# Pool-input products placed inside the attention, pool openings beside products, and another half first in a w_down tile

## The chip, the cores and the metric

The kernel runs on one core of one Trainium2 chip. The metric is device time in microseconds (us), the median of several runs; lower is better. Engines are named as in the profile: PE (TensorE matmul), PEld (TensorE weight load), DVE (VectorE), ACT (ScalarE), POOL (GpSimd), SP (SyncE, which issues the DMAs).

## What is computed

Two layers of a diffusion backbone on 512 latent and 128 context tokens, with the same weights, D_MODEL 1024. The reference, cut to one layer:

```python
def trunk_layer(x, mod, lp, attend):
    h = modulate(rmsnorm(x, lp['g_ffn1']), m[0], m[1])
    x = x + 0.5 * m[2] * swiglu(h, lp['w_ffn1_gate'], lp['w_ffn1_up'], lp['w_ffn1_down'])
    n = modulate(rmsnorm(x, lp['g_mix']), m[3], m[4])
    proj = n @ lp['w_in']
    q, k, v, u_pool, u_conv, gate_b, gate_c, merge = jnp.split(proj, IN_OFFSETS, axis=-1)
    ...
    a = attend(q, k, v).transpose(0, 2, 1, 3).reshape(B, L, ATTN_DIM)
    pl = multiscale_pool(u_pool, lp['w_pool'], lp['pool_scale'])
    cv = gate_b * short_conv(gate_c * u_conv, lp['w_conv'], lp['b_conv'])
    g_a, g_p, g_c = jnp.split(jax.nn.sigmoid(merge), N_BRANCH, axis=-1)
    merged = (g_a * (a @ lp['w_br_attn']) + g_p * (pl @ lp['w_br_pool'])
              + g_c * (cv @ lp['w_br_conv']))
    x = x + m[5] * (merged @ lp['w_out'])
    h = modulate(rmsnorm(x, lp['g_ffn2']), m[6], m[7])
    x = x + 0.5 * m[8] * swiglu(h, lp['w_ffn2_gate'], lp['w_ffn2_up'], lp['w_ffn2_down'])
```

`attend` is a neighbourhood attention with 8 heads of 64 (windows of 8 rows by 16 columns plus 128 cached context keys) for latent tokens, and a full attention over 128 tokens for context. `multiscale_pool` takes means over windows of 2, 4, 8 and 16 tokens; `short_conv` is a depthwise convolution over 3 tokens.

## The kernel before

The body is Python that writes every engine's instruction list by a planner (`Sched`). Strands of work are generators; each `yield ACT(n)`, `PE(n, 3)` and the like asks for an engine with an estimated cost, and the planner grants the request that can start first, and of those the one of the smaller priority number. So the order on each engine is fixed when the program is built; on the chip an instruction waits by semaphores for its data and its buffers only. `yield event` holds a strand in the planner's time. Rings hand out buffers: 8 PSUM banks (`BANK`), 5 temporaries, 4 weight staging buffers (`RAW`), 4 pairs of split weights (`HL`).

All 640 tokens are columns; activations lie as 128 features by 640 tokens. A float32 operand is kept as a high and a low part, and every product is three matmuls (`mm3`, L302 to L304). Weights arrive in pieces of 512 KB over SP and are split into the parts `wh` (ACT, L307) and `wl` (DVE, L310) ahead of use.

The main strand (priority 5) goes through a layer: first FFN in three chunks (`ffn`), token mixing (`mix`), second FFN. In a chunk of `ffn` the gate and up products of 8, 8 and 6 feature tiles come first (`unit`; its products for the first token half, `n21`, end last), then eight w_down tiles (`dn`), each for token half 0 and then half 1; `dn` reads the activations `gh` and `gl` of all the chunk's feature tiles.

`mix` opens a memory pool `att` and starts the attention's strands at priorities about 2: per pair of heads `s_master` transposes q and k (L1344), multiplies scores (L1321, L1322) and starts the softmax (DVE, ACT L1310); `t_master` transposes its rows (L1415, and L1437 for context tokens), and multiplies values (L1326, L1327). Beside them main multiplies the q, k and v columns of w_in, which go through `qk_post` (POOL, L1200 to L1213), and four gate pieces (`xgate_post`). Then main waits until scores, values and copies of all four pairs are through (`yield sm_done`, `yield tm_done`, `at_ev`, `xev`), and `att` closes. Next it opens the pool `pc` and multiplies the eight pieces `u` (pool input), `x`, `c` and `b` (convolution), two of each, of 128 columns of w_in by all tokens, half by half (`gemm`, 384 and 256 tokens). Their results are copied or multiplied out of PSUM (`nat_copy`, `nat_mul`, `conv_out`), and `pool_mean`, `pool_map` and `conv` work on them, mostly on DVE. When these are done (`for ev in done`), `pc` closes and `mrg` opens: sigmoids of the gates (L1746, L1753), six more gate groups (`gate`), branch products, the merge (`br_post`, DVE), and w_out products (`outp`), which read the merged rows `mg`.

`acc` are two tiles of 384 columns in which the norms sum squares (L655).

Of the kernel before, what the change touches and what calls it, by code (L numbers as in the profile page):

```python
# [183 lines left out]
def POOL(n):  # L184
    return ("pool", 0.16 + n * 0.0021)
# [80 lines left out]
def body(ctx: ExitStack, tc: tile.TileContext, a, outs):  # L266
# [20 lines left out]
    small = const.tile([128, 32, 4], F32, name="small")  # L287
    acc = [const.tile([128, 384], F32, name=f"acc{h}") for h in range(2)]

# [541 lines left out]
    def ffn(l, i, ops, close, nxt, nxt_b):  # L831
# [167 lines left out]
        for ci, (c0, c1) in enumerate(CHUNKS):  # L999
            nk = c1 - c0  # L1000
            last = ci == len(CHUNKS) - 1
            gev = [[Ev(), Ev()] for _ in range(nk)]
            for f in range(nk):
                if ci or f >= NW:
                    yield from unit(f, gev[f], f == nk - 1)
                    continue
                w2 = []
                for _ in range(2):
                    w2.append((yield from w_take()))
                done = [S.spawn(whole(h, f, w2, gev[f]), 4 + h + 0.1 * f) for h in range(2)]  # L1010

                def end(w2=w2, done=done, f=f):
                    for ev in done:
                        yield ev
                    for w in w2:
                        w_free(w)
                    S.set(tail[f])

                S.spawn(end(), 0)
            xe, op_n, nt_ev = [[None] * KD] * 2, None, None  # L1020
            halves = HB if nxt_b or not last else HA
            if last and nxt:
                nt_ev = Ev()
                xe, op_n = nxt(nt_ev) if nxt_b else nxt()
            W = []
            for d in range(KD):
                w = yield from w_take()
                yield from dn(w, nk, d, halves[0], gev, xe[0][d])
                if last and d == 0 and nxt_b:

                    for ev in side:
                        yield ev
                    es2.close()
                    np_ = es.enter_context(tc.tile_pool(name="ntmp", bufs=1))
                    nt = [np_.tile([128, 4, 320], F32, name=f"nt{j}") for j in range(4)]
                    S.set(nt_ev, (nt, [t[:, 6:8].rearrange("p a (b t) -> p (a b) t", b=2) for t in g2]))
                if last and d >= 4:
                    W.append(w)
                    continue
                yield from dn(w, nk, d, halves[1], gev, xe[1][d])  # L1040
                w_free(w)
            for d, w in enumerate(W, 4):
                yield from dn(w, nk, d, halves[1], gev, xe[1][d])
                w_free(w)
# [9 lines left out]
    def mix(l, op, nxt):  # L1054
# [8 lines left out]

        with tc.tile_pool(name="att", bufs=1) as tpool:

# [425 lines left out]

            S.spawn(misc(), 2)
            S.spawn(klo_zero(), 2)
            S.spawn(ck_strand(), 2)
# [22 lines left out]
            for w in w1:  # L1517
                w_free(w)
            for u in (1, 2, -1, 3):
                w0 = yield from take2()  # L1520
                for b in range(5):
                    (p,) = yield from b_form(w0, b)
                    if u < 0:
                        S.spawn(v_post(p, 1, b), 2.4)
                    else:
                        S.spawn(qk_post(p, u, b), 2)
                for w in w0:
                    w_free(w)
            xev = []
            for i in range(2):  # L1530
                wait = v_ev[1] if i == 0 else tr_ev[3]
                for c in range(2):
# [5 lines left out]
                    w_free(w)  # L1538
            yield sm_done
            yield tm_done  # L1540
            for p_ in range(4):
                for ev in at_ev[p_]:
                    yield ev
            for ev in xev:
                yield ev

        if True:
            sp = [t[:, SPARE:].rearrange("p (a t) -> p a t", t=NT) for t in NN]
            pl = [sp[0][:, 0:2], sp[0][:, 2:4]]
# [3 lines left out]

            def nat(h, t, p):

                v = t[:, NL0:NL0 + 512].rearrange("p (r j c) -> p j r c", r=8, j=4)
                if h == 0:
                    yield v[:, 0:3], p[:, 0:384].rearrange("p (j r c) -> p j r c", j=3, r=8)
                else:
                    yield v[:, 3], p[:, 0:128].rearrange("p (r c) -> p r c", r=8)  # L1560
                    yield t[:, NC0:NC0 + 128], p[:, 128:256]

            with tc.tile_pool(name="pc", bufs=1) as pc:
                u = pc.tile([128, 2, NAT], F32, name="u")
                xs = pc.tile([128, 2, NAT], F32, name="xs")
# [10 lines left out]
                LO, HI = NC0, NL0 + 512  # L1576
                u_ev = [[Ev(), Ev()] for _ in range(2)]
                x_ev = [[Ev(), Ev()] for _ in range(2)]
# [14 lines left out]

                def pads():
                    yield POOL(200)
                    for t in (u, xs):
                        for c0, c1 in ((0, NC0), (NC0 + 128, NL0), (NL0 + 512, NAT)):
                            nc.gpsimd.memset(t[:, :, c0:c1], 0.0)
                    S.set(pad_ev)

                def nat_copy(dst, p, c, h, ev):
                    yield pad_ev
                    for nv, blk in nat(h, dst[:, c], p):
                        yield ACT(384 if h == 0 else 128)
                        copy(nv, blk)
                    S.give(BANK, p)
                    S.set(ev)

                def nat_mul(p, c, h, ev):
# [7 lines left out]
                def conv_out(p, c, h):  # L1617
                    yield y_ev[c]
                    n = HW[h]
                    t = yield TMP  # L1620
                    for (nv, blk), (_, tblk) in zip(nat(h, u[:, c], p), nat(h, u[:, c], t)):
                        yield DVE(384 if h == 0 else 128)
# [16 lines left out]
                def pool_mean(c):  # L1639
# [4 lines left out]
                    yield ld_ev  # L1644
                    uc = u[:, c]
                    yield from shift_add(s2, uc, 0, 1, NAT, RA)
# [44 lines left out]
                def conv(c):  # L1691
                    for ev in c_ev[c] + pm_ev:
                        yield ev
                    z = xs[:, c]
                    yo = y[:, c, LO:HI]
                    yield DVE(HI - LO)
# [9 lines left out]

                done = []
                S.spawn(loads(), 2)
                S.spawn(pads(), 1)
                for c in range(2):  # L1710
                    S.spawn(pool_mean(c), 2)
                    done.append(S.spawn(pool_map(c), 2))
                    S.spawn(conv(c), 2)
                for kind in "uxcb":
                    for c in range(2):
                        w = yield from w_take()
                        for h in range(2):
                            p = yield BANK
                            yield from gemm(p, w, 0, n2, HA[h], op[h])
                            if kind == "u":  # L1720
                                S.spawn(nat_copy(u, p, c, h, u_ev[c][h]), 2)
                            elif kind == "x":
                                S.spawn(nat_copy(xs, p, c, h, x_ev[c][h]), 2)
                            elif kind == "c":
                                S.spawn(nat_mul(p, c, h, c_ev[c][h]), 2)
                            else:
                                done.append(S.spawn(conv_out(p, c, h), 2))
                        w_free(w)
                for ev in done:
                    yield ev  # L1730

            if True:
                rp = es.enter_context(tc.tile_pool(name="mrg", bufs=1))
                wm0 = cnt["take"]
                items = [(r, hf) for r in ADA[l, "mix"][1] for hf in range(2)]
                side = S.spawn(ada(l, items, rp, lambda j: w_done[wm0 + 30 * j // (8 * len(items))]), 6)
                sg = [rp.tile([128, 2, NT], F32, name=f"sg{i}") for i in range(3)]
                mg = [sp[1][:, 2:6], rp.tile([128, 4, NT], F32R, name="mg1")]
                sga_ev = [Ev(), Ev()]
# [8 lines left out]

                def sg_post(p, dp, i, c, h):
                    if dp:  # L1750
                        yield br_ev[dp - 1][c][h]
# [42 lines left out]
                def branch(w, dp, c, h):  # L1794
                    banks = []
                    for i, (src, k0, nk) in enumerate((((ahi, alo), 0, 4), (pl, 4, 2), (cv, 6, 2))):
# [3 lines left out]
                        banks.append(p)  # L1800
                    S.spawn(br_post(banks, dp, c, h), 2)

# [15 lines left out]

                for i in range(2):
                    S.spawn(sga_sig(i), 2)  # L1820
                for ch in range(2):
                    for dp in (2 * ch, 2 * ch + 1):
                        for i in range(0 if ch else 1, 3):
                            yield from gate(dp, i)
                        w2 = yield from w_take()
                        w2 = [w2, (yield from w_take())]
# [20 lines left out]
                    for d in range(2, KD):  # L1847
                        yield from outp(W[d // 2], ch, d, 1, xe[1][d])
                        if d % 2:
                            w_free(W[d // 2])  # L1850
        return ops, closer(es, [side])

# [156 lines left out]
```

## Time and profile before

| | us |
|---|---|
| median of 3 runs (2840.92 to 2843.91) | 2841.22 |
| the profiled execution | 2841.3 |
| its span, first to last instruction | 2839.5 |
| PE busy | 2763.1 |
| DVE busy | 2106.6 |
| ACT busy | 1238.6 |
| POOL busy | 177.9 |

A busy PE is one that has a matmul in work; matmuls overlap, so starts, not lengths, tell its pace. All times in the views count from the span's start. The granted clock is the share of TensorE's full clock, 1.00 for 2.4 GHz and 0.50 for 1.2.

### The profile page before, as it was taken

What the parts mean: (1) busy time and instruction counts of PE and PEld (TensorE: products, weight loads), DVE (VectorE), ACT (ScalarE), POOL (GpSimd) and SP (SyncE); (2) the same over time, 40 slices, a digit from 0 to 9 for tenths busy, and PEclk for the clock granted to TensorE, in tenths of its full rate; (3) what the DMA queues carried; (4) which work ended last, traced back from release to release, by engine and by line L of the source; (5) the groups of instructions that cost most, each with busy time, mean ns of one, the idle gap of its engine ahead of it and who ended that gap; (6) DMA issues with size and microseconds to landing.
All of it is one profiled execution on the core that took longest, in us unless ns stands there. A gap on an engine that the chain in (4) does not pass through costs nothing.

```text
span 2839.5 us, 48917 instructions
## 1 busy us (share of the span) xinstructions
PE 2763.1 (97%) x19612; PEld 2709.5 (95%) x19612; DVE 2106.6 (74%) x3733; ACT 1238.6 (44%) x2324; POOL 177.9 (6%) x255
## 2 busy tenths in 40 slices
PE   6999999998999999999999999999999999999999
PEld 6999999997999999999999999999889999999999
DVE  7888886886676688888788686777865767856564
ACT  5525244686322364342455252547843223624332
POOL 0000001630000000000000000026300000000000
PEclk9999999998999999999999999999999999999999
DMA  5343423221334224443314233222213332122312
GB/s 216 128 151 108 150 95 106 81 85 57 107 125 140 82 76 153 126 132 129 95 55 143 81 103 114 95 84 88 75 63 131 123 131 71 60 97 67 104 60 90
DMA packets 120020, 296.69 MB, mean 104 GB/s; under 512 B 15088, under 2 KB 23280, under 8 KB 118768
## 3 DMA queue, kind: packets, MB, share of 16 engines
q1 hardware_dynamic: 119792, 293.57, 31.8%
q8 instruction: 153, 2.51, 0.4%
q14 instruction: 75, 0.61, 0.1%
HBM read 289.85 MB, written 3.67 MB: 103 GB/s over the span
## 4 chain that ended last, share of the span: by engine, by line
PE 88%; DVE 5%; ACT 4%; issue 1%; DMA 1%; POOL 0%; SPq 0%; DVEq 0%; ACTq 0%; POOLq 0%
PE b L302 28%; PE b L304 28%; PE b L303 28%; DVE wl L310 1%; DVE nlo L310 1%; PE b L1415 1%; ACT nlo L307 1%; PE b L558 1%; DMA wf<-in_wm_dram 1%; PE b L1327 1%; PE b L1326 0%; ACT P L307 0%; PE b L1322 0%; ACT P L1310 0%; PE b L1321 0%
## 5 line engine op out<-in xcount | busy, mean ns | idle before, releaser
L302 PE MATMUL b<-nhi,wh 128*128 128x320 f32 (+2 forms) x3584 | 1114.3, 311 | 9.8 <-ACT nhi L307 5.7
L303 PE MATMUL b<-nhi,wl 128*128 128x320 f32 (+2 forms) x3584 | 1107.9, 309 | 0.2 <-DVE wl L310 0.2
L304 PE MATMUL b<-nlo,wh 128*128 128x320 f32 (+2 forms) x3520 | 1088.8, 309 | 4.3 <-DVE nlo L310 4.1
L307 ACT ACTIVATE wh<-raw 128x1024 fp32r<-128x1024 f32 (+2 forms) x472 | 457.8, 970 | 592.6 <-PE b L304 527.4
L302 PEld LDWEIGHTS b<-nhi,wh 128*128 128x128 f32 x3584 | 674.2, 188 | 17.2 <-ACT nhi L307 8.2
L303 PEld LDWEIGHTS b<-nhi,wl 128*128 128x128 f32 x3584 | 674.1, 188 | 2.4 <-DVE wl L310 1.8
L310 DVE TENSOR_TENSOR wl<-raw,wh 128x1024 fp32r<-128x1024 f32 (+2 forms) x472 | 529.4, 1122 | 191.1 <-ACT wh L307 189.4
L304 PEld LDWEIGHTS b<-nlo,wh 128*128 128x128 f32 x3520 | 661.9, 188 | 8.1 <-DVE nlo L310 8.0
L302 PE MATMUL b<-gh,wh 128*128 128x320 f32 (+2 forms) x1424 | 443.7, 312 | 0.0
L304 PE MATMUL b<-gl,wh 128*128 128x320 f32 (+2 forms) x1424 | 440.8, 310 | 2.9 <-DVE gl L310 2.9
L303 PE MATMUL b<-gh,wl 128*128 128x320 f32 (+2 forms) x1424 | 439.8, 309 | 0.0
L545 DVE SCALAR_TENSOR_TENSOR ma<-wm,csil,ma 128x512 f32<-128x512 f32 x448 | 315.8, 746 | 6.6 <-DMA wm<-in_wmod_dram 6.5
L304 PEld LDWEIGHTS b<-gl,wh 128*128 128x128 f32 x1424 | 267.8, 188 | 5.2 <-DVE gl L310 4.8
L302 PEld LDWEIGHTS b<-gh,wh 128*128 128x128 f32 x1424 | 267.8, 188 | 3.4 <-issue 3.0
L303 PEld LDWEIGHTS b<-gh,wl 128*128 128x128 f32 x1424 | 267.9, 188 | 0.3
L796 DVE SCALAR_TENSOR_TENSOR x<-b,mh,x 128x128 f32<-128x128 f32 (+3 forms) x288 | 117.7, 436 | 179.9 <-PE b L304 179.6
L307 ACT ACTIVATE f<-b 128x320 f32<-128x320 f32 x240 | 104.6, 437 | 218.9 <-PE b L304 216.7
L898 DVE TENSOR_TENSOR f<-f,b 128x320 f32<-128x320 f32 x240 | 112.4, 483 | 101.8 <-PE b L304 92.8
L302 PE MATMUL b<-wh,nhi 128*128 128x256 f32 x480 | 140.6, 293 | 3.0 <-ACT nhi L712 3.0
L667 POOL TENSOR_TENSOR small<-small,nhalf 128x3 f32<-128x3 f32 (+1 forms) x12 | 12.0, 1001 | 2023.3 <-DVE small L663 2023.3
L303 PE MATMUL b<-wh,nlo 128*128 128x256 f32 x480 | 137.2, 286 | 1.3 <-DVE nlo L718 1.3
L304 PE MATMUL b<-wl,nhi 128*128 128x256 f32 x480 | 136.8, 285 | 0.0
(205 smaller groups left out, 3477.7 us busy)
## 6 DMA issues: line engine op xcount, KB each, us to landing
raw<-in_w_dram SPq DMA_DIRECT2D x280, 512.0 KB, 3.4
wm<-in_wmod_dram SPq DMA_DIRECT2D x256, 256.0 KB, 3.4
raw<-in_w_dram SPq DMA_DIRECT2D x160, 256.0 KB, 2.8
raw<-in_w_dram SPq DMA_DIRECT2D x32, 384.0 KB, 3.1
wf<-in_wm_dram SPq DMA_DIRECT2D x8, 1024.0 KB, 12.1
B<-in_rpb_dram SPq DMA_DIRECT2D x16, 448.0 KB, 3.3
x<-in_xT_dram SPq DMA_DIRECT2D x4, 640.0 KB, 8.7
out_y_dram<-x SPq DMA_DIRECT2D x8, 192.0 KB, 1.9
```

The source lines that it names most:

```text
L302: nc.tensor.matmul(out, lhsT=l2[0], rhs=r2[0], start=first, stop=False, skip_group_check=more)
L303: nc.tensor.matmul(out, lhsT=l2[1], rhs=r2[0], start=False, stop=False, skip_group_check=more)
L304: nc.tensor.matmul(out, lhsT=l2[0], rhs=r2[1], start=False, stop=last, skip_group_check=more)
L307: nc.scalar.activation(out=out, in_=in_, func=AF.Copy, scale=scale)
L310: nc.vector.tensor_tensor(out=out, in0=in0, in1=in1, op=ALU.subtract)
L545: nc.vector.scalar_tensor_tensor(out=ma[g], in0=t, scalar=c, in1=ma[g], op0=ALU.mult, op1=ALU.add)
L558: nc.tensor.matmul(bank[32 * c:32 * c + 32, 0:128], lhsT=sel[:, g, :], rhs=ma[g][:, 128 * c:128 * c + 128], start=(g == 0), stop=(g == 1), ...
L667: nc.gpsimd.tensor_tensor(out=rs[:, :nb], in0=rs[:, :nb], in1=nhalf[:, :nb], op=ALU.pow)
L796: nc.vector.scalar_tensor_tensor(out=x[:, d, s], in0=bank[:, c0:c1], scalar=col[:, d, g:g + 1], in1=x[:, d, s], op0=ALU.mult, op1=ALU.add)
L898: nc.vector.tensor_tensor(out=t, in0=t, in1=bank[:, :320], op=ALU.add)
L1327: nc.tensor.matmul(out, lhsT=v, rhs=pt[1][:, :n], start=False, stop=last)
L1415: nc.tensor.transpose(bank[:, 128 * i:128 * i + 128], P[h, j][:, 128 * s:128 * s + 128], ident)
```

## The change

In `mix`, the two `u` pieces are multiplied by main behind the four gate pieces and ahead of the wait for the attention; their results go to a tile in a pool of its own (`upool`) and to the accumulators of the norms, which become one tile of 768 columns (`accu`). The wait for the attention goes into a strand of its own (`att_end`), and so does the opening of `pc` (`pc_stage`): main goes on with `x`, and stops after its first piece until `pc` is open; what is done to the products waits for the opening too (`pc_post`). The opening of `mrg` is a strand as well (`mrg_stage`); main stops for it after the first gate group, whose sigmoids wait for it. The merge of an odd `dp` gets priority 0.3 instead of 2. In `ffn`, the first w_down tile of every chunk is multiplied for token half 1 first, and then for half 0. The diff, cut:

```diff
-    acc = [const.tile([128, 384], F32, name=f"acc{h}") for h in range(2)]
+    accu = const.tile([128, 768], F32, name="acc")
+    acc = [accu[:, 384 * h:384 * h + 384] for h in range(2)]
...
                 w = yield from w_take()
+                if d == 0:
+                    yield from dn(w, nk, d, halves[1], gev, xe[1][d])
                 yield from dn(w, nk, d, halves[0], gev, xe[0][d])
...
-                yield from dn(w, nk, d, halves[1], gev, xe[1][d])
+                if d:
+                    yield from dn(w, nk, d, halves[1], gev, xe[1][d])
...
+        eu = ExitStack()
+        u = [eu.enter_context(tc.tile_pool(name="upool", bufs=1)).tile([128, NAT], F32, name="u"), accu[:, 0:NAT]]
...
+        def pads(ts, ev):
+            yield POOL(200)
+            for t in ts:
+                for c0, c1 in ((0, NC0), (NC0 + 128, NL0), (NL0 + 512, NAT)):
+                    nc.gpsimd.memset(t[:, c0:c1], 0.0)
+            S.set(ev)
+        def u_pads():
+            for h in range(2):
+                for ev in op[h]:
+                    yield ev
+            yield from pads(u, upad_ev)
...
+            S.spawn(u_pads(), 2)
...
-            yield sm_done
-            yield tm_done
-            for p_ in range(4):
-                for ev in at_ev[p_]:
+            for c in range(2):
+                w = yield from w_take()
+                for h in range(2):
+                    p = yield BANK
+                    yield from gemm(p, w, 0, n2, HA[h], op[h])
+                    xev.append(S.spawn(nat_copy(u[c], p, h, upad_ev, u_ev[c][h]), 3))
+                w_free(w)
+            def att_end():
+                yield sm_done
+                yield tm_done
+                for p_ in range(4):
+                    for ev in at_ev[p_]:
+                        yield ev
+                for ev in xev:
                     yield ev
-            for ev in xev:
-                yield ev
+                ea.close()
+            att_done = S.spawn(att_end(), 0)
...
-            with tc.tile_pool(name="pc", bufs=1) as pc:
-                u = pc.tile([128, 2, NAT], F32, name="u")
+            def pc_stage():
+                yield att_done
+                epc = ExitStack()
+                pc = epc.enter_context(tc.tile_pool(name="pc", bufs=1))
...
+                S.set(pc_open, (epc, post))
+            def pc_post(*args):
+                epc, post = yield pc_open
+                yield from post(*args)
+            S.spawn(pc_stage(), 0)
+            for kind in "xcb":
+                for c in range(2):
+                    w = yield from w_take()
+                    for h in range(2):
+                        p = yield BANK
+                        yield from gemm(p, w, 0, n2, HA[h], op[h])
+                        done.append(S.spawn(pc_post(kind, p, c, h), 2))
+                    w_free(w)
+                    if kind == "x" and c == 0:
+                        epc, _ = yield pc_open
...
+            def mrg_stage():
                 for ev in done:
                     yield ev
+                epc.close()
+                eu.close()
+                rp = es.enter_context(tc.tile_pool(name="mrg", bufs=1))
...
+                for i in range(2):
+                    S.spawn(sga_sig(i), 2)
+                S.set(mrg_open)
...
                 def sg_post(p, dp, i, c, h):
+                    yield mrg_open
...
-                    S.spawn(br_post(banks, dp, c, h), 2)
+                    S.spawn(br_post(banks, dp, c, h), 0.3 if dp % 2 else 2)
...
                         for i in range(0 if ch else 1, 3):
                             yield from gate(dp, i)
+                            yield mrg_open
```

## Rows read from the trace of the kernel before

**Rows 1.** The page, busy time of PE and PEld, share, instructions:

```profile
PE 2763.1 (97%) x19612; PEld 2709.5 (95%) x19612; DVE 2106.6 (74%) x3733; ACT 1238.6 (44%) x2324; POOL 177.9 (6%) x255
```

**Rows 2.** PE's waits, whole span: us in total, times, longest:

```profile
PE b L1415 <- ACT P L307: 11.5, 9, 3.3
...
PE b L1344 <- POOL sga L1213: 6.6, 2, 3.3
...
PE b L304 <- DVE gl L310: 2.9, 7, 0.7
...
PE b L304 <- DVE mg L310: 2.7, 4, 0.9
```

**Rows 3.** Stretches: us, then busy PE, PEld, DVE, ACT, POOL; clock; DMA:

```profile
560.00:640.67 80.67, 80.50 (x606) 78.69 (x606) 67.45 (x160) 69.86 (x185) 35.04 (x51) 1.00 0.26 83
640.67:674.70 34.03, 24.76 (x106) 17.84 (x105) 22.60 (x55) 27.22 (x74) 0.00 (x0) 0.75 0.10 32
...
674.70:740.00 65.30, 65.30 (x447) 65.03 (x447) 39.48 (x56) 25.90 (x45) 0.54 (x8) 1.00 0.28 86
2044.83:2078.62 33.79, 23.66 (x107) 16.66 (x105) 22.70 (x55) 27.23 (x74) 0.00 (x0) 0.85 0.09 32
```

**Rows 4.** PE's groups from 640.67 us: count, busy us, mean ns, idle before:

```profile
L1415 PE MATMUL b<-ident,P 128*128 128x128 f32 x42 | 10.3, 357 | 6.6 <-ACT P L307 5.5 <-ACT Ps L307 1.0
L1326 PE MATMUL b<-PT,nhi 128*128 128x256 f32 (+3 forms) x19 | 8.7, 460 | 1.2 <-ACT PT L307 1.2
```

**Rows 5.** PE's timeline (start, length, instruction): first matmuls of two successive pieces:

```profile
718.85 0.34 PE L302 MATMUL b<-nhi,wh 128*128 128x384 f32 x1
...
725.85 0.34 PE L302 MATMUL b<-nhi,wh 128*128 128x384 f32 x1
```

**Rows 6.** PE's timeline: transposes of softmax rows, and the first u product:

```profile
601.84 0.82 PE L1415 MATMUL b<-ident,P 128*128 128x128 f32 x6
...
610.26 0.38 PE L1437 MATMUL b<-ident,Ps 128*128 128x128 f32 x2
...
623.40 0.60 PE L1415 MATMUL b<-ident,P 128*128 128x128 f32 x4
...
630.46 0.38 PE L1415 MATMUL b<-ident,P 128*128 128x128 f32 x2
...
640.67 1.12 PE L1415 MATMUL b<-ident,P 128*128 128x128 f32 x6
...
648.10 0.38 PE L1437 MATMUL b<-ident,Ps 128*128 128x128 f32 x2
...
655.08 0.47 PE L1415 MATMUL b<-ident,P 128*128 128x128 f32 x1 [3.29 <-ACT P L307]
...
664.65 0.38 PE L1415 MATMUL b<-ident,P 128*128 128x128 f32 x2
...
666.51 1.41 PE L1415 MATMUL b<-ident,P 128*128 128x128 f32 x4 [1.48 <-ACT P L307]
...
673.00 0.38 PE L1437 MATMUL b<-ident,Ps 128*128 128x128 f32 x2
...
674.70 0.39 PE L302 MATMUL b<-nhi,wh 128*128 128x384 f32 x1
```

**Rows 7.** Copies of u out of PSUM, both layers: ns shortest, median, longest:

```profile
L307 ACT ACTIVATE u<-b x12: 272/277/491, 679.2 to 2093.1; 128x128 f32<-128x128 f32 x8, 128x384 f32<-128x384 f32 x4
```

**Rows 8.** ACT's timeline: two successive weight splits, and the first sigmoids of mrg:

```profile
647.66 1.06 ACT L307 ACTIVATE wh<-raw 128x1024 fp32r<-128x1024 f32 x1
...
682.30 1.06 ACT L307 ACTIVATE wh<-raw 128x1024 fp32r<-128x1024 f32 x1
...
735.73 2.62 ACT L1746 ACTIVATE sga<-sga 128x640 f32<-128x640 f32 x4
```

**Rows 9.** POOL's timeline: the memsets of u:

```profile
676.89 0.21 POOL L1598 MEMSET u<- 128x16 f32 x3 [37.38 <-issue]
```

**Rows 10.** Groups, whole span: the norms' adds into acc, mean ns:

```profile
L655 DVE TENSOR_TENSOR acc<-acc,t 128x320 f32<-128x320 f32 (+2 forms) x84 | 41.5, 494 | 25.7 <-ACT t L647 23.7
```

More of the change, by code (lines that the diff above doesn't have):

```diff
@@ L1062, in mix, with nat, nat_copy @@
         at_ev = [[Ev(), Ev()] for _ in range(4)]
-        with tc.tile_pool(name="att", bufs=1) as tpool:
+        eu = ExitStack()
+        u = [eu.enter_context(tc.tile_pool(name="upool", bufs=1)).tile([128, NAT], F32, name="u"), accu[:, 0:NAT]]
+        u_ev = [[Ev(), Ev()] for _ in range(2)]
+        upad_ev = Ev()
+        def nat(h, t, p):
+            v = t[:, NL0:NL0 + 512].rearrange("p (r j c) -> p j r c", r=8, j=4)
+            if h == 0:
+                yield v[:, 0:3], p[:, 0:384].rearrange("p (j r c) -> p j r c", j=3, r=8)
+            else:
+                yield v[:, 3], p[:, 0:128].rearrange("p (r c) -> p r c", r=8)
+                yield t[:, NC0:NC0 + 128], p[:, 128:256]
+        def pads(ts, ev):
[9 more added lines that the diff above has]
+            yield from pads(u, upad_ev)
+        def nat_copy(dst, p, h, pad, ev):
+            yield pad
+            for nv, blk in nat(h, dst, p):
+                yield ACT(384 if h == 0 else 128)
+                copy(nv, blk)
+            S.give(BANK, p)
+            S.set(ev)
+        ea = ExitStack()
+        tpool = ea.enter_context(tc.tile_pool(name="att", bufs=1))
+        if True:
             VC = 5 * 512
@@ L1518, in mix @@
                 w_free(w)
-            for u in (1, 2, -1, 3):
+            for pr in (1, 2, -1, 3):
                 w0 = yield from take2()
@@ L1522, in mix @@
                     (p,) = yield from b_form(w0, b)
-                    if u < 0:
+                    if pr < 0:
                         S.spawn(v_post(p, 1, b), 2.4)
                     else:
-                        S.spawn(qk_post(p, u, b), 2)
+                        S.spawn(qk_post(p, pr, b), 2)
                 for w in w0:
@@ L1538, in mix @@
                     w_free(w)
-            yield sm_done
-            yield tm_done
-            for p_ in range(4):
-                for ev in at_ev[p_]:
+            for c in range(2):
[12 more added lines that the diff above has]
+                for ev in xev:
                     yield ev
-            for ev in xev:
-                yield ev
+                ea.close()
+            att_done = S.spawn(att_end(), 0)
         if True:
+            done = []
+            pc_open = Ev()
             sp = [t[:, SPARE:].rearrange("p (a t) -> p a t", t=NT) for t in NN]
@@ L1552, in mix @@
             cv_e2 = [[Ev(), Ev()] for _ in range(2)]
[L1554 to L1561, printed above, removed]
-            with tc.tile_pool(name="pc", bufs=1) as pc:
-                u = pc.tile([128, 2, NAT], F32, name="u")
+            def pc_stage():
+                yield att_done
+                epc = ExitStack()
+                pc = epc.enter_context(tc.tile_pool(name="pc", bufs=1))
                 xs = pc.tile([128, 2, NAT], F32, name="xs")
@@ L1576, in mix @@
                 LO, HI = NC0, NL0 + 512
-                u_ev = [[Ev(), Ev()] for _ in range(2)]
                 x_ev = [[Ev(), Ev()] for _ in range(2)]
@@ L1592, in loads @@
                     S.set(wp_ev)
[L1594 to L1607, printed above, removed]
                 def nat_mul(p, c, h, ev):
@@ L1620, in conv_out @@
                     t = yield TMP
-                    for (nv, blk), (_, tblk) in zip(nat(h, u[:, c], p), nat(h, u[:, c], t)):
+                    for (nv, blk), (_, tblk) in zip(nat(h, u[c], p), nat(h, u[c], t)):
                         yield DVE(384 if h == 0 else 128)
@@ L1644, in pool_mean @@
                     yield ld_ev
-                    uc = u[:, c]
+                    uc = u[c]
                     yield from shift_add(s2, uc, 0, 1, NAT, RA)
@@ L1694, in conv @@
                     z = xs[:, c]
-                    yo = y[:, c, LO:HI]
+                    yo = y[c][:, LO:HI]
                     yield DVE(HI - LO)
@@ L1705, in conv, with post @@
                     S.set(y_ev[c])
-                done = []
+                def post(kind, p, c, h):
+                    if kind == "x":
+                        return nat_copy(xs[:, c], p, h, pad_ev, x_ev[c][h])
+                    if kind == "c":
+                        return nat_mul(p, c, h, c_ev[c][h])
+                    return conv_out(p, c, h)
                 S.spawn(loads(), 2)
-                S.spawn(pads(), 1)
+                S.spawn(pads([xs[:, c] for c in range(2)], pad_ev), 1)
                 for c in range(2):
@@ L1713, in mix @@
                     S.spawn(conv(c), 2)
[L1714 to L1728, printed above, removed]
+                S.set(pc_open, (epc, post))
@@ L1729, in mix @@
+            mrg_open = Ev()
+            side = []
+            def mrg_stage():
                 for ev in done:
                     yield ev
+                epc.close()
+                eu.close()
+                rp = es.enter_context(tc.tile_pool(name="mrg", bufs=1))
+                items = [(r, hf) for r in ADA[l, "mix"][1] for hf in range(2)]
+                side.append(S.spawn(ada(l, items, rp, lambda j: w_done[wm0 + 30 * j // (8 * len(items))]), 6))
+                sg.extend([rp.tile([128, 2, NT], F32, name=f"sg{i}") for i in range(3)])
+                mg.append(rp.tile([128, 4, NT], F32R, name="mg1"))
+                for i in range(2):
+                    S.spawn(sga_sig(i), 2)
+                S.set(mrg_open)
@@ L1732, in mix @@
             if True:
-                rp = es.enter_context(tc.tile_pool(name="mrg", bufs=1))
                 wm0 = cnt["take"]
[L1735 to L1738, printed above, removed]
+                sg = []
@@ L1739, in mix @@
+                mg = [sp[1][:, 2:6]]
                 sga_ev = [Ev(), Ev()]
@@ L1817, in hand_on @@
                     S.set(nt_ev, (nt, b12))
-                for i in range(2):
-                    S.spawn(sga_sig(i), 2)
+                S.spawn(mrg_stage(), 0)
                 for ch in range(2):
@@ L1850, in mix @@
                             w_free(W[d // 2])
-        return ops, closer(es, [side])
+        return ops, closer(es, side)
     def prep():
```

## The prediction

> **What bounds the kernel now.** I read the busy line of the page first: TensorE (PE) has work in 2763.1 of 2839.5 us [rows 1]. So only two things can shorten this kernel: fewer products, which this change doesn't bring, or less time in which PE has none. Next I read PE's list of waits for who ends its idle time [rows 2]: the largest entry beside the kernel's start is the transposition of the softmax rows (L1415), 11.5 us in 9 waits for ScalarE (ACT). Then I read the table of stretches for where that is [rows 3]. While the attention runs beside other products (560 to 640.67 us) PE is busy in 80.50 of 80.67 us at clock 1.00, with ACT busy in 69.86. From 640.67 us the attention runs alone: in 34.03 us PE is busy in 24.76, at a mean clock of 0.75, so half of that stretch ran at the lower of its two levels (1.2 instead of 2.4 GHz), after PE had stood idle. In layer 1 it is 33.79 us and 23.66. I call these two stretches the tails. From 674.70 to 740 us PE is busy without a break at clock 1.00: neither the opening of the `pc` pool nor that of `mrg` costs PE anything now. What can be won is in the tails, and in some waits of under a microsecond elsewhere.
>
> **How much is empty in a tail.** Its PE work at full clock: 42 transposes of L1415 and 4 of L1437, 128 columns each, 19 value products of L1326 [rows 4] and as many of L1327, 10 score products each of L1321 and L1322; with two left from the gate before, these are the 106 of [rows 3]. The widths are in the code: 1792 columns for one head's values, three heads, and 512 for context tokens, is 5888; 1920 for one head's scores, two heads, is 3840. So 2 x 5888 + 2 x 3840 + 5888 (transposes) = 25,344 columns. A piece (24 matmuls of 384 columns and 24 of 256, 15,360 columns) takes 7.00 us in dense running [rows 5], 0.456 ns a column: 11.6 us. The 58 products of 128 columns go slower: the six transposes at 601.84 us take 0.82 us, the two at 610.26 0.38 [rows 6], so (0.82 - 0.38) / 4 = 0.11 us each instead of 0.058, which adds 58 x 0.05 = 2.9. Work 14.5 us, hole 34.0 - 14.5 = 19.5 us, twice: 39 us is the most that filling the tails can give.
>
> **Pool-input columns in the tail.** Main now issues, ahead of the wait for the attention, the two `u` pieces and the first `x` piece: 3 x 7.00 = 21.0 us of PE work a layer [rows 5], slightly more than the hole. They leave the place after the tail, so a layer gains 34.0 + 21.0 minus the new length T of the tail. T can't be below 14.5 + 21.0 = 35.5 (PE full). I build T from what the last heads do [rows 6]. A head's pass, first transposes to last, takes 7.43 us alone (640.67 to 648.10) and 8.42 beside products (601.84 to 610.26), or 7.06 for the even head (623.40 to 630.46); in the tail the even head takes 9.57 (655.08 to 664.65), at the low clock. Between passes PE waits for ACT's softmax: 6.98 and 1.86. From the last odd head's context transposes to the tail's end 1.70. Now: 8.42 + gap + 7.06 + gap + 8.42 + 1.70. ACT gets more to do before the first gap ends: copies of a `u` half, 0.49 for one of 384 columns and 2 x 0.28 for the other [rows 7], 1.05 a piece, and a weight split of 1.06 [rows 8], so 2.1; in the second gap one piece's copies, 1.05. Gaps 9.1 and 2.9. T = 37.6. Each layer gains 55.0 - 37.6 = 17.4, both 34.8. Between T = 35.5 (39.0) and the bound of the rival below (16.2). The full clock is in it, since passes beside products ran at 1.00 [rows 3].
>
> What else moves with it. The weights of these pieces are at hand: no split stands on ACT between 647.66 and 682.30 us [rows 8], so four pieces lie ready in the four buffer pairs. Freed three pieces sooner, the buffers take three splits and three weight DMAs (SP, 512 KB) into the tail; DMA is busy there in 0.10 of the time [rows 3], and of the splits the sum holds the one that can meet the saturated part. The copies of `u` carry priority 3 behind the attention's 2; what one of them holds up when it is started first is in the gaps. Their six memsets on POOL move to the start of the attention, ahead of QK-norm steps for which PE waits 6.6 us in all (L1344) [rows 2]: three took 0.21 us [rows 9], so 0 to 0.42 a layer; I take 0.4 for both. The four DMAs of the pool branch stay behind the opening of `pc`. The accumulators of the norms become one tile: adds take 494 ns [rows 10], and if a half had to wait for one of the other's, six norms would lose up to 3.0 us; since the halves touch different columns I take 0 and keep 3.0 for the range.
>
> **Pools open beside products.** New waits: main stops after the first `x` piece until `pc` is open, and after the first gate group until `mrg` is open; every later product is queued behind these on PE. They are waits of the planner that writes the order, no semaphores: PE itself is only held by PSUM banks. What covers them: `x` one, `c` two, `b` two, gates two pieces, 7 x 7.00 = 49 us from the end of the tail until the order needs `mrg`. Now the sigmoids that follow the opening start 735.73 - 674.70 = 61 us after the tail [rows 6, 8], 5 us behind 56 us of products; with 21 less ahead, 40 us if VectorE (DVE) keeps up. Its 39.5 us of work in 65.3 [rows 3] would then nearly fill its time. Cover 49: cost 0.
>
> **First w_down tile and branch priority.** At a chunk's end the first w_down product of half 0 waits for the activation that was split last: 2.9 us in 7 waits [rows 2]. Half 1 is ready one product earlier and its own 3.5 us (24 matmuls of 320 columns at 0.456 ns a column) cover the rest: gain 2.9, at least 0, at most 2.9. The merge steps of odd `dp` at priority 0.3 may shorten the 2.7 us of waits for `mg` [rows 2], which end a chain of seven dependent steps; half, 1.4, between 0 and 2.7.
>
> **Sum.** The profiled execution took 2841.3 us (2839.5 span and 1.8 around it), the median of the three runs 2841.22. 34.8 + 2.9 + 1.4 - 0.4 = 38.7, so 2802.6.
>
> **Rivals.** (1) *The products hold up the attention.* PE and ACT keep the order written for them, and a piece's matmuls stand ahead of the transposes and value products that ACT and DVE wait for. Beside products a pair followed the pair before by 37.8 us (610.26 to 648.10), in the tail by 24.9 [rows 6]. At that pace T = 7.4 + 37.8 + 1.7 = 46.9: a layer gains 8.1, both 16.2, in all 20.1: 2821.2. For it: ACT is busy in 27.2 of the 34.0 us even now [rows 3]. Against it: those 37.8 us hold also a next pair's transposes and QK-norm, which the last pair lacks, and the passes themselves were hardly slower (8.42 against 7.43). The Trainium skill says in "TensorE: Matmul & The Clock Gate", part 2, "The MATMULs themselves stay in program order", only weight loads being pulled ahead; a product put into a hole that has closed by then is therefore paid by the attention. By that rule alone this rival would be the result; the trace agrees on the order (at 674.70 us the `u` product starts behind the last value products) but shows dense stretches in which it costs a pass 1 us.
> (2) *Slower: the openings come late.* Place: the DVE chain of pool means, pooled map and convolution, which now has 49 us of products beside it. If `mrg` opens at 61 us as now, PE stops 12 us a layer, 24 in all: 2826.6, still faster. From (38.7 + 5.7) / 2 = 22.2 us of stop, an opening 71 us after the tail, the kernel is slower by over 0.2%; at 75 us it is 2841.3 - 38.7 + 52 = 2854.6. Against it: DVE idles in 26 of the 65 us now, and its list after 674.70 waits mostly for products.
> (3) *It doesn't fill.* Banks or an order that places the pieces behind the attention leave the tails as they are: 2.9 + 1.4 - 0.4 = 3.9, 2837.4, within 0.2%. Against it: the gate pieces just before 640.67 us filled the same kind of hole with 0.17 us idle in 80.
>
> **How the numbers follow.** Forecast 70%, 2793 to 2811 (all bounds at their best: 39.0 + 2.9 + 2.7 = 44.6, 2796.7, and 3 us below for a rearranged order elsewhere; T up to 41 at the other end). Rival 1 20% (2811 to 2824, with the small terms at their worst), rival 3 5%, rival 2 5%. The range 2792 to 2822 leaves out rivals 2 and 3 and a little of the first. A difference of 0.2% (5.7 us) is about what a measurement of this kernel can tell from no change: faster 90%, within 5% (rival 3), slower 5% (rival 2).
>
> **What would show it.** In the changed kernel, PE has no idle stretch of several us between the end of the gate pieces and the `c` pieces, the clock stays at 1.00 but for the tail's last us, the matmuls into `u` start before the last transposes of softmax rows, and the waits for the softmax fall from 11.5 to about 3 us. From the last gate matmul to the last value product it should be 36 to 40 us a layer; 45 or more means rival 1. The sigmoids of `mrg` start about 40 us behind the tail. The waits for `gl` vanish from PE's list. I am wrong if the tail's products are spread so that PE still waits, if `x` holds banks that the attention needs, or if PE waits behind the pools.

## The result, and the profile after

| | before, us | after, us |
|---|---|---|
| median of the runs | 2841.07 | 2797.6 |
| profiled execution | 2841.3 | 2795.04 |
| its span | 2839.5 | 2793.3 |
| PE busy | 2763.1 | 2740.2 |

The ratio is 0.9843, 95% interval 0.9824 to 0.9862: faster by about 44.6 us. One disturbed execution of the changed kernel (4469.1 us) is left out of the ratio; the other three took 2795.04, 2796.31 and 2798.88. The forecast was 2802.6, between 2792 and 2822. Between the two profiled executions the gain is 46.3 us, which the trace places stage by stage.

After, the page's busy line, which answers [rows 1]:

```profile
span 2793.3 us, 48930 instructions
...
PE 2740.2 (98%) x19612; PEld 2700.0 (97%) x19612; DVE 2102.1 (75%) x3733; ACT 1238.1 (44%) x2324; POOL 178.7 (6%) x267
```

The matmuls are as many as before. The span shrank by 46.2 us and PE's busy time by 22.9, so 23.3 us of the gain are idle time that is gone. The busy time fell with as many matmuls since a matmul that stands alone, or at the low clock, is listed with a longer time than one in a dense stretch: the first value product of the last even head, 512 columns, with 0.79 us before (657.56 us, low clock) and 0.39 after (660.20 us).

After, PE's waits over the whole span (us in total, times, longest), against [rows 2]:

```profile
PE b L662 <- DVE acc L657: 11.3, 1, 11.3
PE b L1387 <- POOL sga L1256: 6.6, 2, 3.3
...
PE b L1370 <- DVE PT L312: 1.5, 4, 0.6
...
PE b L1458 <- ACT P L309: 0.3, 2, 0.2
```

The wait for softmax rows (L1458, before L1415) fell from 11.5 us to 0.3, further than the forecast's 3. The lines for `gl` and for `mg` are gone from the list. The wait of the QK-norm transposes (L1387, before L1344) kept its 6.6. The first line is the kernel's start, the one place where PE waits for the norms' adds.

After, the table of stretches (us, then busy PE, PEld, DVE, ACT, POOL; clock; DMA), against [rows 3]; the first line begins at the last transposition of q and k of the last pair, the next two are the tail of each layer, the fourth the time from the tail to the sigmoids of `mrg`:

```profile
631.00:676.50 45.50, 44.52 (x303) 42.37 (x301) 32.70 (x75) 39.10 (x102) 3.85 (x6) 1.00 0.22 69
638.48:676.50 38.02, 37.04 (x251) 34.89 (x249) 26.44 (x57) 31.96 (x83) 0.00 (x0) 1.00 0.22 70
2017.86:2055.87 38.01, 37.03 (x250) 34.89 (x249) 26.43 (x57) 31.95 (x83) 0.00 (x0) 1.00 0.23 70
676.50:716.50 40.00, 40.00 (x271) 39.73 (x271) 34.61 (x53) 17.77 (x32) 0.55 (x8) 1.00 0.24 74
```

A tail now holds 21.0 us of pool-input products as well. It is 4.0 us longer than before and PE is idle in 1.0 of its 38.0 us and the clock is 1.00, the full level; before it was idle in 9.3 of 34.0 at 0.75. The products no longer stand behind it: 34.0 + 21.0 - 38.0 = 17.0 us a layer.

After, PE's timeline of the tail (start, length, instruction), against [rows 6]:

```profile
638.48 0.34 PE L304 MATMUL b<-nhi,wh 128*128 128x384 f32 x1
...
639.00 0.82 PE L1458 MATMUL b<-ident,P 128*128 128x128 f32 x6
...
648.65 0.38 PE L1480 MATMUL b<-ident,Ps 128*128 128x128 f32 x2
...
657.25 0.82 PE L1458 MATMUL b<-ident,P 128*128 128x128 f32 x6
...
664.47 0.41 PE L1458 MATMUL b<-ident,P 128*128 128x128 f32 x2
...
669.54 0.82 PE L1458 MATMUL b<-ident,P 128*128 128x128 f32 x6
...
670.79 0.28 PE L306 MATMUL b<-nlo,wh 128*128 128x256 f32 x1
...
674.80 0.38 PE L1480 MATMUL b<-ident,Ps 128*128 128x128 f32 x2
...
676.50 0.39 PE L304 MATMUL b<-nhi,wh 128*128 128x384 f32 x1
```

The `u` products begin 0.5 us before the first transposes of softmax rows. The last product of the tail starts at 670.79; the 5.7 us from there to the first product behind the tail are the last head's pass with no product left to put beside it.

After, ACT's timeline behind the tail, against the last line of [rows 8]:

```profile
716.54 2.62 ACT L1804 ACTIVATE sga<-sga 128x640 f32<-128x640 f32 x4
```

The sigmoids start 40.0 us behind the tail, as forecast, and before PE has come to the end of the 49 us of products ahead of them.

### The profile page after: what moved, and what is told of

Same layout as the page of the kernel before. It is cut to its first block, busy times and chain, and to the rows that moved or that the text cites. A ratio compares the mean times of both kernels' runs of the same rounds, so it can differ in the third digit from the quotient of the medians.

```text
span 2793.3 us, 48930 instructions
## 1 busy us (share of the span) xinstructions
PE 2740.2 (98%) x19612; PEld 2700.0 (97%) x19612; DVE 2102.1 (75%) x3733; ACT 1238.1 (44%) x2324; POOL 178.7 (6%) x267
## 3 DMA queue, kind: packets, MB, share of 16 engines
q1 hardware_dynamic: 119792, 293.57, 32.4%
## 4 chain that ended last, share of the span: by engine, by line
PE 92%; DVE 4%; ACT 2%; issue 1%; DMA 1%; POOL 0%; SPq 0%; DVEq 0%; ACTq 0%; POOLq 0%
PE b L304 29%; PE b L306 29%; PE b L305 29%; DVE wl L312 1%; PE b L1458 1%; DVE nlo L312 1%; PE b L560 1%; DMA wf<-in_wm_dram 1%; PE b L1365 1%; PE b L1370 1%; PE b L1364 1%; PE b L1369 0%; DVE t L690 0%; ACT nlo L309 0%; PE b L1387 0%
```

## The experiments

All differences below are ratios times the kernel before (2841 us), with the 95% interval of the ratio. Stages are compared by landmarks of PE: the last transposes of q and k, the first product behind the tail, the first product of w_down and of w_out.

**Half 1 first in the first w_down tile, alone** (`dn_only`: the kernel before with this edit):

```diff
                 w = yield from w_take()
+                if d == 0:
+                    yield from dn(w, nk, d, halves[1], gev, xe[1][d])
                 yield from dn(w, nk, d, halves[0], gev, xe[0][d])
...
-                yield from dn(w, nk, d, halves[1], gev, xe[1][d])
+                if d:
+                    yield from dn(w, nk, d, halves[1], gev, xe[1][d])
```

> The kernel before with one part of the change: half 1 first in a chunk's first w_down tile. By the terms of the prediction it gains 2.9 us (the idle time that PE's list of waits gives to gl), so 2838.1 against 2841.1. By the stage times of the changed kernel, where eight w_down starts and what precedes them are 0.1 to 0.9 us shorter, it gains about 5.4 us: 2835.7. Both say that no wait for gl is left.

Measured: 2836.53 us, ratio 0.9983 (0.9974 to 0.9992), 4.8 us. The prediction took 2.9, and called that the most. The interval is 2.3 to 7.4 us, so the times alone don't tell 4.8 from 2.9; the traces do. One of the seven waits in the kernel before shows it; PE's timeline:

```profile
147.92 0.31 PE L302 MATMUL b<-gh,wh 128*128 128x320 f32 x1
148.06 0.31 PE L303 MATMUL b<-gh,wl 128*128 128x320 f32 x1
148.81 0.41 PE L304 MATMUL b<-gl,wh 128*128 128x320 f32 x1 [0.43 <-DVE gl L310]
149.05 0.31 PE L302 MATMUL b<-gh,wh 128*128 128x320 f32 x1
```

The list of waits counts 0.43 us here, from the end of one matmul to the start of the next. Without the wait the next would have started 0.147 us after the one before (the pace of the lines around), not after its 0.31 us: the start is 0.75 - 0.147 = 0.60 late, and the one after that another 0.10 (149.05 - 148.81 = 0.24). Summed in this way over the seven waits, what PE lost is 4.8 us. In the trace of `dn_only` these seven places are together 4.9 us shorter: the edit gave all of it back.

**Priority of the odd merges, alone** (`br_only`):

```diff
-                    S.spawn(br_post(banks, dp, c, h), 2)
+                    S.spawn(br_post(banks, dp, c, h), 0.3 if dp % 2 else 2)
```

> The kernel before with one part of the change: priority 0.3 for the merge of an odd dp. By the terms of the prediction 1.4 us (half of the 2.7 us of waits for mg), so 2839.7. By the stage times of the changed kernel (four w_out stretches each 1.13 to 1.15 us shorter) 4.6 us: 2836.5. A rival: those 4.6 us come from the other openings of the pools, and then this kernel gains nothing.

Measured: 2836.4 us, ratio 0.9983 (0.9974 to 0.9992), 4.8 us. Here too the interval (2.3 to 7.4 us) holds the upper bound of the forecast, 2.7, and the traces have to decide. From the first w_out products to the next norm the trace is shorter by 1.14 + 1.15 us in each layer, 4.6 in all. Not half of the listed 2.7 us but all of them went, and the late starts with them. PE's timeline before, one of the four waits:

```profile
824.22 0.28 PE L303 MATMUL b<-nlo,wl 128*128 128x256 f32 x1
825.37 0.39 PE L304 MATMUL b<-mg,wh 128*128 128x256 f32 x1 [0.88 <-DVE mg L310]
825.60 0.28 PE L302 MATMUL b<-nlo,wh 128*128 128x256 f32 x1
```

Counted from start to start, the next one's late start included, the four cost 3.7 us. A shorter stop 1 us ahead of two of them (0.41 us from start to start at 968.89 us, where the pace is 0.148), which the list of waits doesn't name, makes 0.7 of the rest.

**The mixing part alone** (`mix_only`: the changed kernel without these two edits):

```diff
-                if d == 0:
-                    yield from dn(w, nk, d, halves[1], gev, xe[1][d])
...
-                if d:
-                    yield from dn(w, nk, d, halves[1], gev, xe[1][d])
+                yield from dn(w, nk, d, halves[1], gev, xe[1][d])
...
-                    S.spawn(br_post(banks, dp, c, h), 0.3 if dp % 2 else 2)
+                    S.spawn(br_post(banks, dp, c, h), 2)
```

> The changed kernel without the w_down order and without the new priority: the pool-input columns, the first x piece and the openings alone. If the parts add up (5.4 and 4.6 us for the two left out, 46.3 in all) it gains 35 to 36 us: 2805 to 2806. If the openings beside products are what shortens the w_out stretches, it gains about 41: 2800.

Measured: 2806.22 us, ratio 0.988 (0.9867 to 0.9894), 34.1 us; by the medians measured with it 35.2. With the two small parts 34.1 + 4.8 + 4.8 = 43.7, against 44.6 for the whole change: the parts add up, and each stands where its stage is.

**Only the `u` pieces in the tail** (`u_only`: main waits for the pool ahead of `x`, not behind its first piece):

```diff
             S.spawn(pc_stage(), 0)
+            epc, _ = yield pc_open
             for kind in "xcb":
...
-                    if kind == "x" and c == 0:
-                        epc, _ = yield pc_open
```

> The changed kernel, but main stops for the opening of pc ahead of the first x piece: 14 us of products in a tail instead of 21. If the gain is the filling of holes (19.5 us a layer, of which the changed kernel fills 17), 14 us of products fill somewhat under 14 and the tail is 34 to 36 us long: a layer loses 3 to 5 us against the changed kernel, 2802 to 2806. If the gain came from the clock alone (the chain of the attention at 2.4 instead of 1.2 GHz, whatever fills), 14 us would give nearly the same as 21: 2796 to 2799.

Measured: 2810.51 us, ratio 0.99 (0.9884 to 0.9915), 28.4 us: further from the change than I had expected, and not near the 2796 to 2799 of a gain by the clock alone. PE's stretches from the last transposes of q and k to the first product behind the tail, and from 659.59 us, where the products are used up:

```profile
630.74:676.85 46.11, 41.63 (x255) 37.64 (x253) 31.80 (x75) 38.04 (x101) 3.85 (x6) 0.89 0.17 57
659.59:676.85 17.26, 12.79 (x55) 9.27 (x54) 10.79 (x24) 12.01 (x32) 0.00 (x0) 0.70 0.18 62
```

With 14 us of products the stretch is 46.1 us, with 21 (the change) it is 45.5. The third piece cost the tail nothing, where the two `u` pieces had made it longer (46.1 us against 674.70 - 633.19 = 41.5 in the kernel before): it went into time in which PE otherwise idles 4.5 us and has a mean clock of 0.70. It is worth its 7.0 us and 0.6 more, 7.6 (7.2 in layer 1).

**The products ahead of the attention** (`u_first`: main has priority 1 instead of 5 for the `u` pieces and the first `x` piece, so that the planner prefers them to the attention's 2):

```diff
+            mine = S.cur
+            mine.prio = 1
             for c in range(2):
                 w = yield from w_take()
...
                     if kind == "x" and c == 0:
+                        mine.prio = 5
                         epc, _ = yield pc_open
```

> The changed kernel with the same pieces in the tail, but with priority 1 for them on PE instead of 5, so that they go ahead of the attention's transposes and value products instead of into their holes. If it is the holes that pay, the attention is held up by what it had run beside: the tail gets several us longer (up to 21 a layer if nothing overlaps), 2800 to 2835. If the place alone pays (the pieces are off the path once they stand in the tail), it is the same: 2796.

Measured: 2828.98 us, ratio 0.996 (0.9945 to 0.9975), 11.4 us, hardly more than the 9.6 of the two small parts. The same three pieces in the same place of the program, ahead of the same wait, give next to nothing (1.6 and 0.5 us in the two layers) when they don't stand in the holes. The table of stretches from the last transposes of q and k, cut where the passes begin:

```profile
631.91:660.39 28.48, 28.48 (x199) 28.48 (x197) 11.14 (x22) 15.09 (x36) 3.85 (x6) 1.00 0.29 91
660.39:692.82 32.43, 23.98 (x107) 17.52 (x105) 21.45 (x54) 24.57 (x66) 0.00 (x0) 0.79 0.06 17
```

In the first 28.5 us PE is full, but 195 of its 199 matmuls are products; the rest are the last two transposes of q and k, a value product of the head before and, at the end, the first transposition of softmax rows, and not one score product is among them. So ACT, which makes the softmax, has work in 15.1 us only; its listed waits there, 7.4 us, are for the products' own results. Then comes the tail of [rows 3] once more, 32.4 us with 24.0 busy at clock 0.79. In all 60.9 us, 15.4 more than in the changed kernel. In layer 1 it is 61.7 against 45.5. Less the 7.5 us that stand ahead of the tail in the changed kernel (631.00 to 638.48 us), that is a T of 53.4: the sum with T = 46.9 of rival 1 (the products hold up the attention) was not even the worst that this rival can do. The Trainium skill's sentence in "TensorE: Matmul & The Clock Gate", part 2, "The MATMULs themselves stay in program order", describes it; the trace agrees, with 28.48 of 28.48 us full of products, and scores and passes behind them.

**Both `x` pieces in the tail** (`x_both`) **and `c` too** (`c_too`: the same line with `kind == "c" and c == 0`):

```diff
-                    if kind == "x" and c == 0:
+                    if kind == "x" and c == 1:
                         epc, _ = yield pc_open
```

> The changed kernel, but main stops for the opening of pc only after the second x piece, so 28 us of products stand in a tail instead of 21. The tail of the changed kernel still has PE without products for 5.6 us at its end (670.90 to 676.50 us in layer 0). If holes there are all that is left, the second x piece takes them: up to 2.5 us a layer, 2791 to 2795 against 2796. If the four banks that x then holds until the opening starve the attention, the tail gets longer by more than the piece brings: 2797 to 2810.

> The changed kernel, but main stops for the opening of pc only after the first c piece: 35 us of products for a tail, and up to six of the eight PSUM banks held until the opening. Holes left in the tail are 2 to 3 us a layer, so more than the second x piece brings can't be won. If banks are the limit, the attention is starved in the last passes: 2800 or more. If not, as with two x pieces: 2791 to 2795.

Measured: `x_both` 2791.76 us, ratio 0.9829 (0.9816 to 0.9843), 48.6 us; `c_too` 2789.65 us, ratio 0.9827 (0.9812 to 0.9843), 49.1 us, just under the 2791 expected. The stretches of `x_both`, from the last transposes of q and k, and its last pass:

```profile
633.63:683.00 49.37, 49.37 (x344) 48.47 (x343) 33.06 (x76) 39.17 (x102) 3.85 (x6) 1.00 0.20 64
672.17:683.00 10.83, 10.83 (x80) 10.67 (x79) 5.63 (x9) 4.75 (x9) 0.00 (x0) 1.00 0.29 97
```

PE is never idle in this tail. 42 of the 48 matmuls of the second `x` piece went in, 6.3 us (a piece's 7.00 less six matmuls of 256 columns at 0.12), and the stretch grew by 49.37 - 45.50 = 3.87: 2.4 us won a layer, the first piece that is paid in part. In `c_too` the stretch is 49.37 too, and no product of `c` stands ahead of its end. So the holes end here. By the ratios both kernels beat the changed one by some 4 to 5 us, but the intervals of the ratios overlap (0.9816 to 0.9843, against 0.9824 to 0.9862); what shows it is the trace.

**The opening of `mrg` ahead of the first gate group** (`mrg_first`):

```diff
                         for i in range(0 if ch else 1, 3):
-                            yield from gate(dp, i)
                             yield mrg_open
+                            yield from gate(dp, i)
```

> The changed kernel, but main stops for the opening of mrg ahead of the first gate group, with 35 us of products between the tail and that point instead of 49. If the branch chain (pool means, convolution, its products) ends about 40 us behind the tail, as predicted, PE stands idle about 5 us a layer: 2801 to 2810. If DVE needs longer (the second rival), up to 20 us a layer: 2810 to 2840. If the opening is early or PE's order hides it, nothing: 2796.

Measured: 2795.73 us, ratio 0.9847 (0.9832 to 0.9863): the same as the change. I had expected a loss, and that expectation fell. The table of stretches from the end of its tail:

```profile
678.48:740.00 61.52, 61.52 (x418) 61.25 (x418) 43.65 (x66) 25.64 (x45) 0.55 (x8) 1.00 0.29 95
```

The sigmoids start at 718.50, 40.0 us behind this tail, and only the 35 us of the second `x`, the `c` and the `b` pieces stand ahead of the opening in main's list. Still PE doesn't stop: the first gate product starts at 715.62 us, 2.9 us ahead of the sigmoids. Main's `yield mrg_open` holds the planner's time alone; a gate product needs a PSUM bank and its weights, not the pool. So it makes no measurable difference whether this wait stands ahead of the gate group or behind it. No run opens `mrg` in the main strand, as the kernel before does, so what the strand itself is worth is not shown.

## Why the prediction was right, and where its steps were off

**The mechanism held.** What can be won is in the tails; three pieces nearly fill them; the clock stays full; the pool openings cost nothing. 17.0 and 16.7 us a layer came from there (from the last transposes of q and k to the first w_out product, layers 0 and 1), 33.7 in all, where the forecast had 34.8.

**T = 37.6 was measured as 38.0, by errors that cancel.** The terms, in the order of the sum, from the timeline above, each counted to the next row:

| | first odd pass | gap | even pass | gap | last odd pass | end |
|---|---|---|---|---|---|---|
| forecast | 8.42 | 9.1 | 7.06 | 2.9 | 8.42 | 1.70 |
| measured | 9.65 | 8.60 | 7.22 | 5.07 | 5.26 | 1.70 |

(The measured tail has 0.5 us more, since it begins with the first `u` product.) The single errors are +1.23, -0.50, +0.16, +2.17, -3.16 and 0, in all -0.10: that T came out so close is luck. The first odd pass has 33 matmuls of products in it, where the one that the sum took it from (601.84 to 610.26 us) had 24. The even pass took 7.22 us beside products at full clock, where it took 9.57 alone [rows 6], at a mean clock of 0.65 (655.08 to 666.51 us): that step was right. The last odd pass was not "beside products": the last product starts 1.25 us after it begins, so PE is free for it and it takes 5.26; in `x_both`, with products beside it, it takes 8.56, near the 8.42 of the sum. PE's timeline of `x_both`, the passes' starts and the last one's context transposes:

```profile
659.88 0.81 PE L1458 MATMUL b<-ident,P 128*128 128x128 f32 x6
...
672.17 0.82 PE L1458 MATMUL b<-ident,P 128*128 128x128 f32 x6
...
680.73 0.38 PE L1480 MATMUL b<-ident,Ps 128*128 128x128 f32 x2
```

The gap before it was put too short by 2.2. Taken from the start of the even pass to the start of the last one, the two kernels are closer: 11.43 us before and 12.29 after, 0.86 more, and in `x_both`, with products all along as well, 12.29 again. In `u_only`, where the products end 2.4 us behind the start of the even pass, it is 10.21 us, and PE waits for softmax rows at its end:

```profile
656.99 0.82 PE L1458 MATMUL b<-ident,P 128*128 128x128 f32 x6
...
667.20 0.48 PE L1458 MATMUL b<-ident,P 128*128 128x128 f32 x1 [2.09 <-ACT P L309]
```

In the changed kernel PE doesn't wait there: ACT has written the last of these rows by 668.57 us, 1.0 us before the pass starts, behind products. So the softmax sets how early the last pass can start, and the products that the planner put before it set the rest. A gap is what the pass ahead of it leaves of that time; to add a pass and a gap as two terms hid this. What sets ACT's pace there no run took apart.

**w_down: 2.9 forecast, as an upper bound, 4.8 measured; merge: 1.4 forecast, with 2.7 as the upper bound, 4.8 measured** alone (4.6 in its stages). Both steps took the idle time of the list of waits [rows 2] for the time lost. The matmul before a wait is pipelined: its listed length of 0.31 us is twice the pace of 0.147, and that difference, and the slower restart, come on top of each idle entry, some 0.26 us. For the 11 listed waits that is 2.9 us, and 0.7 are the stops that the list doesn't name. And of the merge I took half, with no row that says half; the priority took the waits away wholly.

**The memsets: 0.4 us of loss forecast, none seen.** The wait of L1344 is 6.6 us before and after. The norms' single accumulator, for which 3.0 us stood in the range, shows nothing either: the one wait of PE for these adds is 11.3 us, and 11.5 in the trace of before, and the adds take 494 ns in both.

**The sum.** 33.7 + 4.8 + 4.6 = 43.1 of the 46.3 between the two profiled executions. Of the rest 1.0 us is the clock of one trace, not the change: near 1001 us the kernel before has eight matmuls at 0.267 us each which run at 0.147 in the changed one, and in `dn_only`, which has the same instructions there. Some 2 us I can't assign; the ratio of the runs gives 44.6, not 46.3.

**The rivals.** Rival 1 exists, and the order decides on it: `u_first` made it real and lost nearly the whole gain of the tails. It did not come, as the planner at priority 5 gives the products only the time that the attention leaves. Rival 2 rested on a stop of PE behind the pool's opening. `mrg_first` shows that the order alone does not cause one at 40.0 us; an opening 71 us behind the tail, from which the rival would have been slower, was not tried. Rival 3 fell with the first line of the tail.

## What to carry to other kernels

Count what a stretch has empty (its length less its PE work at full clock), find independent products that stand behind it, and move about that many in at the lowest priority: here 21.0 us of pieces made the tail 4.0 us longer while there were holes, the next 6.3 us made it 3.9 longer, and ahead of the dependent chain the same 21.0 us cost nearly all of their length. When a wait between pipelined matmuls goes away, price it from start to start, not by the idle time that a list of waits shows. What holds a planner's strand isn't what holds the engine: look for the semaphore before a pool's opening is given a cost.

## What the runs showed of the hardware

An idle entry ahead of a matmul is not what the wait costs. Seven waits listed with 2.9 us cost 4.8, since a matmul of 320 columns is listed with 0.31 us while the next can start 0.147 behind it, and the second start after a wait comes 0.10 later than the pace. The clock also doesn't fall alike in all traces. After the same wait of 0.42 us the matmuls of 320 columns followed each other at 0.267 us in the profiled execution of the kernel before (granted clock 0.52 from 1000.45 to 1003.20 us, so nearly all of it at the lower level, after PE had been idle in 0.58 of 1.45 us), and at 0.147 in that of the changed one (clock 1.00), as in all eight other traces. The lines of before, then those of after:

```profile
1000.45 0.54 PE L304 MATMUL b<-nlo,wh 128*128 128x320 f32 x1 [0.42 <-DVE nlo L310]
1000.78 0.47 PE L302 MATMUL b<-nhi,wh 128*128 128x320 f32 x1
1001.05 0.47 PE L303 MATMUL b<-nhi,wl 128*128 128x320 f32 x1
...
978.99 0.41 PE L306 MATMUL b<-nlo,wh 128*128 128x320 f32 x1 [0.42 <-DVE nlo L312]
979.24 0.31 PE L304 MATMUL b<-nhi,wh 128*128 128x320 f32 x1
979.38 0.31 PE L305 MATMUL b<-nhi,wl 128*128 128x320 f32 x1
979.53 0.31 PE L306 MATMUL b<-nlo,wh 128*128 128x320 f32 x1
```

Single differences of about 1 us between two traces of this kernel should be looked at for that before they are laid to an edit.
